# A two-layer decoder trunk on one core: the last tiles, the final norm and the stores by halves of the tokens, and two intermediates kept in PSUM

## Chip, cores, metric

One core of a Trainium2 chip runs the whole program in one launch. The metric is the device time in microseconds, median of three runs.

## What is computed

Two decoder layers over 512 tokens of width 1024, in float32. Each layer is: RMS norm, one input projection, a token mixer beside a memory cross-attention, an output projection added to x, then RMS norm, a SwiGLU feed-forward (width 2816), added to x. A final RMS norm ends it. The parts that the change touches:

```
# lightning indexer of layer 0: one score per query and key, from 8 index heads
logits = einsum('bthd,bsd->bths', q_idx, k_idx)          # 64 wide, after rope
score  = einsum('bths,bth->bts', relu(logits), w_idx)    # then causal mask, top-k keys per query
# rope on the first 16 of 64 features of queries and keys
rot = concat([x1*c - x2*s, x1*s + x2*c])
# feed-forward of the last layer and the end
x = x + (silu(g) * u) @ w_down
y = x * rsqrt(mean(x*x) + eps) * final_norm
```

## The kernel before

Features lie on the 128 partitions, tokens along the free axis: x is eight tiles of 128x512 that stay in SBUF. A matmul in full precision is three passes of a split operand (`mm3`, L169 to L171: high x high, high x low, low x high). Every weight piece is loaded on SP's queue into a ring of four raw buffers, rounded to its high part by ScalarE (`copy`, L148) or VectorE, and its low part is subtracted by VectorE (L163) or GpSimd (L81, in pieces of 256 columns); rings of three high and three low pieces hold the result (`weight`, L157).

**The order.** A string of words per layer (`SEQ`) says in what order units are emitted, and a table (`PLAN`) names for each stage which of the engines takes the next operation of a kind ("V" VectorE, "P" GpSimd, "A" ScalarE). From that the framework builds each engine's queue with a simulated timeline: it may move instructions forward, high-priority ones first, where buffers are free. PSUM tiles of 512 columns are given out by tags with a limit each: "mm" 2, "S" 2, "T" 4, "O" 2. Projections take "mm" and "O" in turn, index tiles "S" and "mm" in turn.

**The start (to about 200 us).** Layer 0 projects four pairs of index queries and the index key, ropes them (`rope`, L309), splits them into stacks (L333), and for each pair of heads and each block of 128 queries multiplies by the keys into PSUM (L633, L634). ScalarE applies relu from PSUM into an SBUF buffer (L636), and VectorE multiplies by the head's weight and adds to the score in SBUF (L641 for the first head, L643). Each of the four pairs makes five PSUM tiles and six multiply-adds, 24 in all, a third each of 256, 384 and 512 columns. When the scores are complete GpSimd multiplies them by the norm's row, and the top-k runs on VectorE: sixteen rounds per block of "eight largest" (L617) and "replace them" (L618), emitted in portions between the other units. The remaining projections, the memory attention and the DSA attention heads follow (L364, L369, L375, L402, L425). Rope shuffles the PSUM result into an SBUF tile b (L312), multiplies the PSUM result by the cosine into a (L313), b by the sine (L314), and adds b to a (L315); the last two go to VectorE or GpSimd by the plan. There are 19 ropes: five in stage 0 with both on VectorE, six in stage 1 with the sine product on GpSimd, eight in layer 1.

**The end.** The second half of layer 1's feed-forward ends with eight down tiles d: 33 matmuls of 512 columns each over eleven activation tiles into one bank (L603), VectorE adds the bank to x (L605), and `absorb` squares the tile and adds the squares up (L215). After the eighth, `final` sums the squares over the partitions with matmuls of one column (L193), makes the inverse root in 13 small VectorE steps (L197 to L205), spreads the column back over the partitions by transposes into PSUM (L212), and for each of eight tiles multiplies x by gain and row (L1014, VectorE) and stores 256 KB (L1015, SP).

Of the kernel before, what the change touches and what calls it, by code (L numbers as in the profile page):

```python
# [11 lines left out]
F32R = mybir.dt.float32r  # L12
I32 = mybir.dt.int32
AF = mybir.ActivationFunctionType
# [16 lines left out]
DOWN_SPLIT = (6, 5)  # L31
BUFS = {"xs": 17, "p": 10, "u": 8, "q": 12, "z": 2, "q1": 8, "qi": 4, "cy": 2, "k": 8, "m": 6, "r": 3, "t": 6, "o": 26, "o2": 6}
RINGS = {"wr": 4, "wh": 3, "wl": 3}
# [32 lines left out]
def r32(ap):  # L66
    return ap.bitcast(F32)
# [25 lines left out]
class Trunk:  # L93
# [215 lines left out]
    def rope(self, ps, tabs, out=None):  # L309
        nc = self.nc  # L310
        a, b = self.slot("t", "ra") if out is None else out, self.slot("t", "rb")
        nc.vector.stream_shuffle(b, ps, SWAP)  # L312
        nc.vector.tensor_mul(a, ps, tabs[0])  # L313
        self.engine("rmul").tensor_mul(b, b, tabs[1])  # L314
        self.engine("radd").tensor_add(a, a, b)  # L315
        return a
# [259 lines left out]
    def ffn(self, i):  # L576
        nc, io = self.nc, self.io
        xs, row = self.xs, None
        for half in range(2):
            acts = []  # L580
            for e in range(NFF // 2):
# [13 lines left out]
                acts.append((hi, lo))  # L595
            for d in range(KC):
                ps = self.ps("mm")
                k = 0
# [7 lines left out]
                if half:  # L606
                    self.absorb(d, 1 if i == 0 else None)


# [14 lines left out]
    def index(self, qs, j, ki, wi, score, first):  # L624

        nc = self.nc
        for heads, b in (((0, 1), 1), ((0,), 2), ((1,), 2), ((0,), 3), ((1,), 3)):
# [3 lines left out]
            for at, e in enumerate(heads):  # L631
                q = qs[e][:, b * P : (b + 1) * P]
                nc.tensor.matmul(ps[:, at * n : at * n + n], q, ki[0][:, :n], start=True, stop=False)  # L633
                nc.tensor.matmul(ps[:, at * n : at * n + n], q, ki[1][:, :n], start=False, stop=True)  # L634
            r = self.slot("u", "relu")
            nc.scalar.activation(r[:, : len(heads) * n], ps[:, : len(heads) * n], AF.Relu)  # L636
# [370 lines left out]

    def final(self):
        nc = self.nc
        with self.tc.high_priority():  # L1010
            row = self.spread(self.rsqrt_mean(self.sums, D, NB), NB)
        for c in range(KC):
            o = self.slot("p", "out")
            nc.vector.scalar_tensor_tensor(o, self.x[c], self.gains[:, 6 * KC + c : 6 * KC + c + 1], row, op0=ALU.mult, op1=ALU.mult)  # L1014
            nc.sync.dma_start(self.io["out"][:, c, :], o)  # L1015

    def run(self):
        self.turn, self.flip, self.comp, self.two, self.ready = False, False, {}, {}, set()
        self.whole = [0] * KC
        self.beside = []  # L1020
        self.plan(0)
        self.setup()
        self.dsa()
        self.ffn(0)
        self.nsa()
        self.ffn(1)
        self.final()

# [77 lines left out]
```

## Time and profile before

| | |
|---|---|
| median of three runs | 1307.31 us (1306.09 to 1307.83) |
| the profiled execution | 1306.26 us, its span 1304.5 us |
| mean granted TensorE clock | 0.971 |
| busy, share of the span | TensorE 95%, VectorE 51%, ScalarE 42%, GpSimd 61% |
| DMA | 108.45 MB, mean 83 GB/s |

The profile is of one execution. Busy time is a sum over stages with different limits; a change is to be judged in its own stage. An engine's waits are put down to what released them. L81 is the helper through which GpSimd's operations go, so these are told apart by their tiles: `stay` weights, `sa` and `sb` stacks, `sc` scores.

### The profile page before, as it was taken

What the parts mean: (1) busy time and instruction counts of PE and PEld (TensorE: products, weight loads), DVE (VectorE), ACT (ScalarE), POOL (GpSimd) and SP (SyncE); (2) the same over time, 40 slices, a digit from 0 to 9 for tenths busy, and PEclk for the clock granted to TensorE, in tenths of its full rate; (3) what the DMA queues carried; (4) which work ended last, traced back from release to release, by engine and by line L of the source; (5) the groups of instructions that cost most, each with busy time, mean ns of one, the idle gap of its engine ahead of it and who ended that gap; (6) DMA issues with size and microseconds to landing.
All of it is one profiled execution on the core that took longest, in us unless ns stands there. A gap on an engine that the chain in (4) does not pass through costs nothing.

```text
span 1304.5 us, 17090 instructions
## 1 busy us (share of the span) xinstructions
PE 1238.6 (95%) x5872; PEld 1024.9 (79%) x5872; DVE 663.2 (51%) x1437; ACT 545.8 (42%) x1053; POOL 801.3 (61%) x1103
## 2 busy tenths in 40 slices
PE   7996889999999999999998998999999999999996
PEld 5775756888888888888887778888788888888885
DVE  6999967543222122223588999997632210122213
ACT  4434678433222222233147767776332322222220
POOL 9988875576553355547466455334886655666573
PEclk9997889999999999999997999999999999999998
DMA  7222000332323433223332101112233323333221
GB/s 246 77 81 80 26 8 23 103 101 94 98 78 89 130 102 97 83 78 99 101 114 65 33 17 52 31 35 81 80 113 97 87 79 119 103 97 93 77 89 65
DMA packets 39239, 108.45 MB, mean 83 GB/s; under 512 B 4720, under 2 KB 8432, under 8 KB 39152
## 3 DMA queue, kind: packets, MB, share of 16 engines
q1 hardware_dynamic: 39152, 107.36, 26.4%
q8 instruction: 46, 0.75, 0.2%
q14 instruction: 41, 0.34, 0.1%
HBM read 105.25 MB, written 2.10 MB: 82 GB/s over the span
## 4 chain that ended last, share of the span: by engine, by line
PE 66%; DVE 21%; POOL 5%; ACT 4%; issue 4%; DMA 0%; DVEq 0%; SPq 0%; POOLq 0%; ACTq 0%
PE ps L171 20%; PE ps L170 20%; PE ps L169 20%; POOL sq L81 2%; DVE p L369 2%; PE ps L425 2%; DVE p L393 2%; DVE sc L618 2%; DVE stay L617 2%; DVE ul L411 2%; POOL stay L81 1%; PE ps L402 1%; ACT p L375 1%; DVE sc L643 1%; DVE rb L312 1%
## 5 line engine op out<-in xcount | busy, mean ns | idle before, releaser
L81 POOL TENSOR_TENSOR stay<-stay,stay 128x256 fp32r<-128x256 f32 (+2 forms) x639 | 471.2, 767 | 312.0 <-ACT stay L148 150.0
L148 ACT CAST stay<-stay 128x1024 fp32r<-128x1024 f32 (+4 forms) x218 | 199.2, 915 | 519.7 <-PE ps L170 400.0
L169 PE MATMUL ps<-xh,stay 128*128 128x512 f32 x912 | 358.6, 393 | 6.1 <-ACT xh L230 6.1
L171 PE MATMUL ps<-xh,stay 128*128 128x512 f32 x912 | 358.8, 394 | 1.0 <-DVE stay L163 0.8
L170 PE MATMUL ps<-xl,stay 128*128 128x512 f32 x912 | 358.5, 394 | 1.0 <-DVE xl L231 1.0
L169 PEld LDWEIGHTS ps<-xh,stay 128*128 128x128 f32 x912 | 173.3, 190 | 41.9 <-ACT xh L230 6.1
L171 PEld LDWEIGHTS ps<-xh,stay 128*128 128x128 f32 x912 | 173.1, 190 | 37.7 <-DVE stay L163 1.9
L170 PEld LDWEIGHTS ps<-xl,stay 128*128 128x128 f32 x912 | 173.1, 190 | 37.1 <-DVE xl L231 1.5
L171 PE MATMUL ps<-fh,stay 128*128 128x512 f32 x352 | 137.1, 389 | 0.0
L170 PE MATMUL ps<-fl,stay 128*128 128x512 f32 x352 | 137.1, 389 | 0.0
L169 PE MATMUL ps<-fh,stay 128*128 128x512 f32 x352 | 137.1, 389 | 0.0
L591 DVE TENSOR_TENSOR fa<-fa,ps 128x512 f32<-128x512 f32 x44 | 30.2, 687 | 183.2 <-PE ps L171 170.6
L605 DVE TENSOR_TENSOR stay<-stay,ps 128x512 f32<-128x512 f32 x32 | 22.1, 690 | 168.4 <-PE ps L171 168.4
L588 DVE TENSOR_TENSOR fa<-ps,row 128x512 f32<-128x512 f32 x44 | 30.2, 691 | 127.2 <-PE ps L171 115.5
L375 ACT ACTIVATE p<-p,stay 128x384 f32<-128x384 f32 (+3 forms) x144 | 80.3, 561 | 34.4 <-DVE stay L369 33.6
L81 POOL TENSOR_TENSOR fa<-fa,row 128x256 f32<-128x256 f32 x88 | 65.7, 768 | 24.1 <-ACT fa L589 24.0
L169 PEld LDWEIGHTS ps<-fh,stay 128*128 128x128 f32 x352 | 66.1, 188 | 13.7
L170 PEld LDWEIGHTS ps<-fl,stay 128*128 128x128 f32 x352 | 66.1, 188 | 13.7
L171 PEld LDWEIGHTS ps<-fh,stay 128*128 128x128 f32 x352 | 66.1, 188 | 13.6
L411 DVE TENSOR_TENSOR ul<-ps,uh 128x512 fp32r<-128x512 f32 (+1 forms) x103 | 62.4, 620 | 12.3 <-ACT uh L410 11.6
L163 DVE TENSOR_TENSOR stay<-stay,stay 128x1024 fp32r<-128x1024 f32 (+4 forms) x38 | 46.4, 1223 | 26.9 <-ACT stay L148 26.1
L410 ACT CAST uh<-ps 128x512 fp32r<-128x512 f32 (+1 forms) x103 | 53.5, 533 | 14.8 <-PE ps L402 13.8
(265 smaller groups left out, 2051.9 us busy)
## 6 DMA issues: line engine op xcount, KB each, us to landing
stay<-in_wf SPq DMA_DIRECT2D x88, 512.0 KB, 3.6
stay<-in_w SPq DMA_DIRECT2D x26, 512.0 KB, 3.5
stay<-in_wd SPq DMA_DIRECT2D x32, 384.0 KB, 3.1
stay<-in_wd SPq DMA_DIRECT2D x32, 320.0 KB, 2.9
mem<-in_memT SPq DMA_DIRECT2D x12, 256.0 KB, 4.0
stay<-in_wo SPq DMA_DIRECT2D x6, 512.0 KB, 3.6
stay<-in_wo SPq DMA_DIRECT2D x16, 192.0 KB, 2.4
stay<-in_xT SPq DMA_DIRECT2D x8, 256.0 KB, 6.2
```

The costliest lines, as they stand in the source:

```text
L81: op(out[:, sl], x[:, sl], y[:, sl])
L148: self.nc.scalar.copy(out, x)
L163: self.engine("w").tensor_sub(lo, raw, r32(hi))
L169: mm(out, lhs[0], rhs[0], start=start, stop=False)
L170: mm(out, lhs[0], rhs[1], start=False, stop=False)
L171: mm(out, lhs[1], rhs[0], start=False, stop=stop)
L369: nc.vector.tensor_tensor_reduce(out=p[:, sl], in0=ps[:, sl], in1=bias, op0=ALU.add, op1=ALU.min, scale=-0.125, scalar=3e38, accum_out=lea ...
L375: self.nc.scalar.activation(p, p, AF.Exp, scale=-1.0, bias=least, accum_out=total)
L410: nc.scalar.copy(hi, ps[:, :w])
L411: nc.vector.tensor_sub(lo, ps[:, :w], r32(hi))
L588: nc.vector.tensor_mul(a, g, row)
L591: nc.vector.tensor_mul(a, a, u)
```

## The change

`rope` multiplies by the cosine first. Where the plan gives the sine product to VectorE, the shuffle writes back into the PSUM tile, the product is made from PSUM, in place if VectorE also adds, else into an SBUF tile. Where it is GpSimd's, only the order of the first two instructions changes. The indexer's relu writes back into its PSUM tile, and VectorE reads it there.

The down tiles 6 and 7 of the last half go through `down_last`: their weights are both prepared first (the second tile's into buffers of their own), then for each half of 256 tokens both tiles are multiplied with 256 columns, added, squared on ScalarE; the half's norm follows, and four products of two tiles each, from gained copies `xg` of x that ScalarE has made tile by tile. In the first half three of these are GpSimd's (`LAST`), which takes the row from a copy in SBUF; in the second all four are VectorE's. Each is stored on SP's queue, 128 partitions x 2 tiles x 256 tokens.

```diff
+HALVED = 2
+LAST = ("PPVP", "VVVV")
     def rope(self, ps, tabs, out=None):
-        a, b = self.slot("t", "ra") if out is None else out, self.slot("t", "rb")
-        nc.vector.stream_shuffle(b, ps, SWAP)
+        a = self.slot("t", "ra") if out is None else out
+        mul, add = self.pick("rmul"), self.pick("radd")
         nc.vector.tensor_mul(a, ps, tabs[0])
-        self.engine("rmul").tensor_mul(b, b, tabs[1])
-        self.engine("radd").tensor_add(a, a, b)
+        if mul == "V":
+            nc.vector.stream_shuffle(ps, ps, SWAP)
+            b = ps if add == "V" else self.slot("t", "rb")
+            nc.vector.tensor_mul(b, ps, tabs[1])
+        else:
+            b = self.slot("t", "rb")
+            nc.vector.stream_shuffle(b, ps, SWAP)
+            self.pool.tensor_mul(b, b, tabs[1])
+        (nc.vector if add == "V" else self.pool).tensor_add(a, a, b)
...
-            r = self.slot("u", "relu")
+            r = ps
             nc.scalar.activation(r[:, : len(heads) * n], ps[:, : len(heads) * n], AF.Relu)
...
             for d in range(KC):
+                if i and half and d == KC - HALVED:
+                    self.down_last(acts)
+                    break
...
+                    if i:
+                        self.last_gain(d, slice(0, S))
+    def last_gain(self, c, sl):
+        if c == 0:
+            self.xg = [self.slot("xg", "xg", w=2 * S).rearrange("p (e t) -> p e t", e=2) for _ in range(KC // 2)]
+        self.nc.scalar.activation(self.xg[c // 2][:, c % 2, sl], self.x[c][:, sl], AF.Copy, scale=self.gains[:, 6 * KC + c : 6 * KC + c + 1])
+    def down_last(self, acts):
+        nc, cs, ws = self.nc, range(KC - HALVED, KC), []
+        for c in cs:
+            k = 0
+            ws.append([])
+            for m in DOWN_SPLIT:
+                if c == cs[0]:
+                    w = self.weight(self.io["wd"][1, 1, c, :, k * P : (k + m) * P], m * P)
+                else:
+                    raw, hi, lo = next(self.rings["wr"])[:, : m * P], *(self.slot("xg", "wx", F32R, 2 * S)[:, : m * P] for _ in range(2))
+                    nc.sync.dma_start(raw, self.io["wd"][1, 1, c, :, k * P : (k + m) * P])
+                    nc.scalar.copy(hi, raw)
+                    self.pool.tensor_sub(lo, raw, r32(hi))
+                    w = hi, lo
+                ws[-1] += [tuple(t[:, e * P : (e + 1) * P] for t in w) for e in range(m)]
+                k += m
+        sq = [self.slot("t", "sq") for c in cs]
+        for h in range(2):
+            sl = slice(h * NM, (h + 1) * NM)
+            for c in cs:
+                ps = self.ps("mm")[:, :NM]
+                for n, w in enumerate(ws[c - cs[0]]):
+                    self.mm3(ps, w, tuple(t[:, sl] for t in acts[n]), n == 0, n == NFF // 2 - 1)
+                with self.tc.high_priority():
+                    nc.vector.tensor_add(self.x[c][:, sl], self.x[c][:, sl], ps)
+                    nc.scalar.activation(sq[c - cs[0]][:, sl], self.x[c][:, sl], AF.Square)
+                    self.last_gain(c, sl)
+            with self.tc.high_priority():
+                row = self.spread(self.rsqrt_mean([t[:, sl] for t in self.sums + sq], D, 2), 2)
+            flat = self.slot("r", "row")[:, :NM]
+            for m in sorted(range(KC // 2), key=lambda m: LAST[h][m], reverse=True):
+                o = self.slot("p", "out").rearrange("p (e t) -> p e t", e=2)
+                wide = lambda t: t[:, None, :].to_broadcast([P, 2, NM])
+                if LAST[h][m] == "V":
+                    nc.vector.tensor_mul(o, self.xg[m][:, :, sl], wide(row))
+                else:
+                    if LAST[h].index("P") == m:
+                        nc.scalar.copy(flat, row)
+                    nc.gpsimd.tensor_mul(o, self.xg[m][:, :, sl], wide(flat))
+                nc.sync.dma_start(self.io["out"][:, 2 * m : 2 * m + 2, sl], o)
-    def final(self):
...
```

The old `final`, shown above, goes.

## Rows read from the trace of the kernel before

**Rows 1.** The page's slices of the span (40 of 32.6 us each, busy share in tenths), TensorE and VectorE.

```profile
PE   7996889999999999999998998999999999999996
...
DVE  6999967543222122223588999997632210122213
```

**Rows 2.** Busy time of each engine in four stretches: us from the span's start, length, then PE, PEld, DVE, ACT, POOL busy (with instruction counts), the granted TensorE clock, DMA share, GB/s.

```profile
27.00:75.00 48.00, 44.57 (x208) 35.81 (x209) 45.98 (x84) 20.49 (x37) 42.57 (x45) 0.93 0.22 67
...
75.00:107.00 32.00, 31.93 (x146) 25.52 (x145) 32.00 (x109) 9.59 (x13) 30.03 (x43) 1.00 0.29 90
...
107.00:170.00 63.00, 47.05 (x237) 37.90 (x236) 62.47 (x171) 39.58 (x121) 55.15 (x87) 0.84 0.14 47
...
200.00:1200.00 1000.00, 978.14 (x4692) 817.29 (x4691) 468.17 (x972) 418.43 (x784) 567.85 (x767) 0.99 0.27 84
```

**Rows 3.** The chain of work that ended last, of the stretch 27 to 170 us alone: shares by engine and line.

```profile
by line: DVE sc L618 17.4%; DVE stay L617 16.0%; DVE sc L643 8.6%; issue 7.7%; DVE ml L231 4.8%; DVE p L369 4.3%; DVE ra L315 4.0%; DVE rb L312 3.6%; DVE stay L510 3.4%; DVE ra L313 3.4%; DVE stay L381 3.2%; DVE stay L163 2.3%; DVE mkl L480
```

**Rows 4.** VectorE's instructions between 20 and 75 us by line and shape: line, operation, out<-in, shapes, count | busy us, mean ns | idle before.

```profile
L643 DVE SCALAR_TENSOR_TENSOR sc<-relu,stay,sc 128x512 f32<-128x512 f32 x7 | 7.6, 1087 | 0.0
...
L643 DVE SCALAR_TENSOR_TENSOR sc<-relu,stay,sc 128x384 f32<-128x384 f32 x7 | 5.9, 840 | 0.0
...
L643 DVE SCALAR_TENSOR_TENSOR sc<-relu,stay,sc 128x256 f32<-128x256 f32 x7 | 5.3, 761 | 0.2
...
L314 DVE TENSOR_TENSOR rb<-rb,sin 128x512 f32<-128x512 f32 x5 | 5.0, 1009 | 0.0
...
L315 DVE TENSOR_TENSOR ra<-ra,rb 128x512 f32<-128x512 f32 x4 | 4.6, 1146 | 0.0
...
L312 DVE STREAM_SHUFFLE rb<-ps 128x512 f32<-128x512 f32 x5 | 3.7, 740 | 0.0
...
L641 DVE TENSOR_SCALAR sc<-relu,stay 128x512 f32<-128x512 f32 x1 | 1.0, 956 | 0.0
...
L641 DVE TENSOR_SCALAR sc<-relu,stay 128x384 f32<-128x384 f32 x1 | 0.9, 891 | 0.0
...
L641 DVE TENSOR_SCALAR sc<-relu,stay 128x256 f32<-128x256 f32 x1 | 0.8, 782 | 0.0
...
L315 DVE TENSOR_TENSOR kk<-kk,rb 128x512 f32<-128x512 f32 x1 | 0.7, 666 | 0.0
```

**Rows 5.** VectorE's instructions of the same kinds between 0 and 180 us that have one operand in PSUM (ps, spread), columns as before.

```profile
L313 DVE TENSOR_TENSOR ra<-ps,cos 128x512 f32<-128x512 f32 x4 | 2.7, 672 | 0.0
...
L497 DVE SCALAR_TENSOR_TENSOR mv<-ps,stay,mv 128x256 fp32r<-128x256 f32 x2 | 0.8, 452 | 0.0
...
L706 DVE SCALAR_TENSOR_TENSOR rw<-rw,stay,spread 128x512 f32<-128x512 f32 x1 | 0.7, 739 | 0.0
```

**Rows 6.** Waits between 27 and 170 us: who waited for whom: us in total, times, longest.

```profile
POOL sc L81 <- DVE sc L643: 4.5, 2, 3.4
...
PE ps L633 <- POOL sb L81: 1.5, 2, 1.2
```

**Rows 7.** TensorE's timeline between 64 and 114 us: start, us, line, operation, shape [idle before it <- releaser].

```profile
69.20 0.43 PE L212 MATMUL spread<-stay 128*128 128x128 f32 x2 [0.40 <-DVE stay L205]
...
113.19 0.58 PE L364 MATMUL ps<-kh,sa 128*128 128x256 f32 x1 [5.91 <-POOL sa L81]
```

**Rows 8.** TensorE's timeline: 256-column matmuls in sequence around 153 us, then the last 512-column matmuls of the last down tile and the column sums behind them.

```profile
152.88 0.28 PE L170 MATMUL ps<-stay,mh 128*128 128x256 f32 x1
...
153.47 0.28 PE L169 MATMUL ps<-stay,mh 128*128 128x256 f32 x1
...
1288.06 0.39 PE L169 MATMUL ps<-fh,stay 128*128 128x512 f32 x1
...
1289.19 0.39 PE L171 MATMUL ps<-fh,stay 128*128 128x512 f32 x1
...
1289.42 0.72 PE L193 MATMUL ssq<-stay,sq 128*128 128x1 f32 x6
```

**Rows 9.** Timeline of all engines after the last down tile.

```profile
1289.62 0.69 DVE L605 TENSOR_TENSOR stay<-stay,ps 128x512 f32<-128x512 f32 x1 [6.79 <-PE ps L171]
...
1290.42 0.63 ACT L221 ACTIVATE sq<-stay 128x512 f32<-128x512 f32 x1 [11.73 <-DVE stay L605]
...
1291.10 1.05 PE L193 MATMUL ssq<-stay,sq 128*128 128x1 f32 x8 [0.74 <-ACT sq L221]
...
1292.19 0.17 DVE L197 TENSOR_SCALAR ssq<-ssq 128x4 f32<-128x4 f32 x1 [1.89 <-PE ssq L193]
...
1294.82 1.11 PE L212 MATMUL spread<-stay 128*128 128x128 f32 x4 [2.67 <-DVE stay L205]
...
1295.97 5.36 DVE L1014 SCALAR_TENSOR_TENSOR out<-stay,spread 128x512 f32<-128x512 f32 x8 [1.21 <-PE spread L212]
```

**Rows 10.** The two nearest rows for a 256-column half: a VectorE addition out of PSUM (L766) and a ScalarE pass out of PSUM (L290): count: ns min/median/max, first and last start, shape.

```profile
L766 DVE TENSOR_TENSOR ho<-ho,ps x24: 395/419/426, 148.6 to 245.6; 64x256 f32<-64x256 f32 x24
...
L290 ACT COPY stay<-spread x1: 374/374/374, 69.7 to 69.7; 128x256 f32<-128x256 f32 x1
```

**Rows 11.** GpSimd's timeline: the last weight piece of the kernel.

```profile
1279.48 1.86 POOL L81 TENSOR_TENSOR stay<-stay,stay 128x256 fp32r<-128x256 f32 x3
```

**Rows 12.** One microsecond while the output is stored, and one while weights in runs of 1 KB are loaded for the last output projection, columns as in Rows 2.

```profile
1299.00:1300.00 1.00, 0.00 (x0) 0.00 (x0) 1.00 (x3) 0.00 (x0) 0.00 (x0) 0.50 1.03 381
...
900.00:901.00 1.00, 1.00 (x8) 0.87 (x7) 0.67 (x1) 0.30 (x1) 0.64 (x2) 1.00 1.07 379
```

More of the change, by code (lines that the diff above doesn't have):

```diff
@@ L31 @@
 DOWN_SPLIT = (6, 5)
-BUFS = {"xs": 17, "p": 10, "u": 8, "q": 12, "z": 2, "q1": 8, "qi": 4, "cy": 2, "k": 8, "m": 6, "r": 3, "t": 6, "o": 26, "o2": 6}
+HALVED = 2
+LAST = ("PPVP", "VVVV")
+BUFS = {"xs": 17, "p": 10, "u": 8, "q": 12, "z": 2, "q1": 8, "qi": 4, "cy": 2, "k": 8, "m": 6, "r": 3, "t": 6, "o": 26, "o2": 6, "xg": 8}
 RINGS = {"wr": 4, "wh": 3, "wl": 3}
@@ L1006, in nsa_second @@
                 self.weighted(o[:, kb * P :], self.vals[:, 2 * br + g, kb], [t[:, cs] for t in parts], br == 0 and kb == 0, False)
-    def final(self):
[L1009 to L1015, printed above, removed]
     def run(self):
@@ L1026, in run @@
         self.ffn(1)
-        self.final()
 def _tiles(w, groups):
```

## The prediction, made before the changed kernel was run

> **What bounds the kernel now.** I read the slices of the page first, then the busy time by stage, the chain of waits of the stretch that stands out, VectorE's instructions there by shape, and last the timeline of the end.
>
> TensorE is full nearly everywhere; VectorE is full only at the start and in the middle [rows 1]. By stages: between 200 and 1200 us TensorE works 978 of 1000 us, so nothing that another engine saves there can show. Between 27 and 170 us VectorE works 45.98 of 48, 32.00 of 32 and 62.47 of 63 us, while TensorE is idle for 3.4, 0.1 and 16 us and its granted clock is 0.84 in the last part [rows 2]. The chain of waits of that stretch names VectorE: the top-k steps (L617, L618), the index accumulation (L643), rope (L312 to L315) [rows 3]. So the first 170 us hang on VectorE's queue and the rest on TensorE, except the end, where each engine waits for the one before it: 11.8 us from the last matmul to the last output multiplication, and 3.2 more to the end of the span at 1304.5 [rows 9].
>
> **Part one: relu and rope in PSUM.** Line 315 shows what is at stake: one addition of two SBUF tensors, 128x512, took 666 ns once and 1146 ns as the mean of four others [rows 4], in a stretch where GpSimd is busy 42.57 of 48 us [rows 2]. With one operand in PSUM the same shape took 672 ns as the mean of four in that stretch (L313) [rows 5]. So an operand in PSUM costs next to nothing of its own and spares what GpSimd's work beside it adds.
>
> *Rope.* In stage 0, five ropes have both choices on VectorE. Their L314 goes from 5.0 to 5 x 0.672 = 3.4 us and their L315 from 4.6 + 0.7 = 5.3 to 3.4: 3.5 us less. The shuffle (five of 740 ns [rows 4]) now writes back into PSUM. No row shows that; between an operation of 672 ns and twice a shuffle I take 740, which it resembles most, so 0. Stage 1's ropes multiply on GpSimd and only change the order of two VectorE instructions: 0. Layer 1's ropes lie where TensorE is 978 of 1000 us busy: 0; without that cover the six that multiply on VectorE would be worth some tenths each.
>
> *Index.* The 21 accumulations cost 7.6 + 5.9 + 5.3 = 18.8 us and the three first multiplications 2.7 [rows 4]. The same instruction with a PSUM operand took 739 ns for 512 columns and 452 for 256 [rows 5]; half way, 600 for 384. New sum: 7 x (0.739 + 0.600 + 0.452) = 12.5, and 1.8 for the three: 7.2 us less. Bounds: 0, if this form does not profit as L313 does; 9, if every one came down to L313's rate of 672 ns for 512 columns. ScalarE's relu writes PSUM instead of SBUF, off the chain: 0.
>
> So VectorE's queue gets 10.7 us shorter before 75 us. The rows put a PSUM operand 6 ns above an SBUF one (672 against 666). [...]
>
> *How much of 10.7 arrives.* Index scores, top-k and the later ropes wait in VectorE's queue, which has no idle time until 170 us, so its work ends 10.7 us earlier if its inputs come. TensorE's part from 75 to 107 us is dense and moves only by the waits before it, 1.5 us for GpSimd's stacks [rows 6]. Then it stands still for 5.91 us for a stack of GpSimd until 113.19 [rows 7]. So TensorE can go on 5.9 + 1.5 = 7.4 us earlier at most. GpSimd, busy 30.03 of 32 us between 75 and 107 [rows 2], waited 4.5 us for the scores of L643 [rows 6]; those it gets back, more only if its contended work shrinks too. Between 4.5 and 7.4 I take 6.0. Bounds: 1.5 (TensorE's waits alone) and 10.7 and about 1.6 more, should the slow matmuls after 113 us vanish (L364, 256 columns, took 0.58 there [rows 7] against 0.28 for as many columns at 153 us [rows 8], and the granted clock of the part is 0.84 [rows 2]).
>
> **Part two: the end by halves.** *Added before the last matmul, on TensorE:* the 66 matmuls of two tiles become 132 of 256 columns. Five steps of the small form took 153.47 - 152.88 = 0.59 us, 0.118 each; five of the large one 1.13, 0.226 each [rows 8]. So 66 x (2 x 0.118 - 0.226) = 0.7 us. The first half's column sums stand in TensorE's queue between the matmuls: three tensors, two blocks, two passes, 12 x 0.12 (six took 0.72 [rows 8]) = 1.4, and two transposes 0.3 (two took 0.43 at 69 us [rows 7]). Together 2.4 us. Behind each of them the second half's matmuls queue up, and everything after waits for these: a stall costs its whole length. Bounds: 0, and 0.74 + 2.67 = 3.4, the two waits at the end today, where nothing covers them [rows 9]. Amid other matmuls the same transposes waited 0.40 us [rows 7]; I take 0.4.
>
> *Removed after the last matmul:* the addition 0.69 to 0.42 and the square 0.63 to 0.37 [rows 9, 10]; the sums from 8 steps to 4, 1.05 to 0.53; the norm's 13 small steps stay; the transposes from four to two, 1.11 to 0.56; the output from eight multiplications to four, 5.36 to 2.68 [rows 9]. Together 4.3 us.
>
> *Covered:* the first half's outputs run beside the second half's 7.8 us of matmuls, three on GpSimd, which has nothing to do after 1281.3 us [rows 11], and their stores go ahead of the others on SP's queue. ScalarE's gain passes (eight tiles) and the second tile's weight casts lie in a stretch where it is a fifth busy; the tile's weights are needed some 4 us earlier, and have buffers of their own instead of waiting for the ring. If GpSimd is late with them, the price is a stall of up to that. The stores have runs of 1 KB instead of 2 KB: the outgoing stream moves 381 GB/s now, and a load with runs of 1 KB moved 379 [rows 12], so 0; bound: 2.7 us if the last megabyte went at half that rate.
>
> Net: 2.4 + 0.4 - 4.3 = -1.5 us, with ends at +1.5 and -1.9 without the store's bound.
>
> **Sum.** The profiled execution took 1306.26 us (1304.5 of span and 1.8 around it): 1306.26 - 6.0 - 1.5 = 1298.8. It lay 1.05 under the median of 1307.31, so as a median 1299.8.
>
> **The rivals.**
> *GpSimd and TensorE keep the pace.* The 75 to 107 us part is full on both [rows 2], and VectorE merely finishes early and idles. Against it: the top-k steps alone are a third of the chain [rows 3] and need no one but VectorE. The front then gives 1.5 and the end, with a stall of both waits' half, 0.2: 1307.31 - 1.7 = 1305.6.
>
> *PSUM does not spare anything.* L643 and the ropes take as long as before, because it is the other operand that waits. Against it: L313 stood at 672 in the midst of the same stretch [rows 5]. Only the end's 1.5 is left: 1305.8.
>
> *PSUM banks run out (slower).* The index tiles were free as soon as ScalarE had read them; now each is held until VectorE's last accumulation on it, and the ropes hold a projection's bank for four instructions instead of two. Twenty index tiles share two "S" and two "mm" banks, and the next projections need "mm" too. VectorE's 14.3 us of index work amid its other work up to 71 us is spread over some 24 us, 1.2 us a tile; if 16 tiles each stop TensorE for that, it loses 19 us, reaches the point at 107 us at about 125 and goes on there 11 to 12 us later than at 113.19. 1307.31 + 11.5 - 1.5 = 1317. It decides once TensorE loses over 7.4 us between 43 and 70 us; below that the wait of 5.91 us and the 1.5 absorb it, and slower by what can be told needs some 12. For it: TensorE has only 3.4 us of room in this stretch [rows 2]. Against it: there are projections to slip in between, and VectorE drains faster than before.
>
> **How the numbers follow.** My forecast 0.55 (its own range 1293 to 1304), pace kept 0.22, nothing spared 0.06, banks 0.09, and 0.08 for more than I forecast, all 10.7 and the vanished slow matmuls and the end at its best: 1307.31 - 12.3 - 1.9 = 1293.1 and below. A measurement of this kernel can tell about 0.2%, 2.6 us: faster is under 1304.7. Faster: 0.54 of the forecast, 0.09 of the pace case, 0.08: 0.71. Same: 0.01, 0.13 and 0.06: 0.20. Slower: 0.09. The range leaves out the bank case and the tail of the best one: 1292.5 to 1307.0.
>
> **What would show it.** L643 at 450 to 740 ns by shape and rope's L314 and L315 successors near 672 beside a busy GpSimd; the first top-k step near 64 to 67 instead of 74.3 us; TensorE's wait at 107 us gone or at 2 us; the end of TensorE's dense part otherwise as it is. At the end: 256-column matmuls every 0.118 us, waits of under 1 us at the first half's sums and transposes, last matmul to last output 7.5 us instead of 11.8. It is wrong if VectorE shows idle time before 170 us, if TensorE waits for VectorE at index or projection matmuls before 70 us, or if the matmuls of the second half stand behind the first half's norm for more than 2 us.

## The result and the profile after

The changed kernel takes 1291.97 us (median of 4 runs, 1291.63 to 1294.74) against 1306.7 for the kernel before (4 runs on the same chip, 1305.81 to 1307.83): ratio 0.9891, 95% interval 0.987 to 0.9911. That is 14.7 us, twice the 7.5 us that were forecast, and 0.5 us below the range. The direction was right; where the time came from was partly not.

The profiled execution of after took 1294.74 us, its span 1292.9 against 1304.5. So 11.6 us can be located in the traces; another 3 lie in which executions were profiled (after's was 2.8 above its median).

The page's slices of after, TensorE and VectorE, as [rows 1]:

```profile
PE   7997878999999999999998899999999999999996
...
DVE  6699976632221122223588999997631210111113
```

The stretches of [rows 2] in after, same columns:

```profile
27.00:75.00 48.00, 46.70 (x222) 38.88 (x222) 37.98 (x100) 22.75 (x39) 40.35 (x53) 0.93 0.25 78
75.00:107.00 32.00, 29.43 (x136) 23.77 (x135) 32.00 (x104) 10.55 (x14) 30.53 (x43) 1.00 0.28 82
107.00:170.00 63.00, 49.95 (x267) 39.26 (x267) 62.50 (x171) 42.88 (x130) 57.13 (x94) 0.92 0.14 43
200.00:1200.00 1000.00, 980.60 (x4708) 820.59 (x4709) 457.31 (x952) 412.29 (x760) 566.64 (x762) 0.99 0.28 84
```

VectorE is now busy for 37.98 of 48 us in the first stretch, where it was 45.98; TensorE rose from 44.57 to 46.70 there. But fixed windows hide where time is won, because everything after slides. Cut both traces at the same instructions instead: the scaling of the index weights (L680, once), the first product of the first gated layer (L588), layer 1's unfolding (L787), the last output-projection addition of layer 1 (L572), and the last product of the second gated layer. I call the stretches start, **front**, first feed-forward, **middle** (layer 1's mixer) and second feed-forward. First the kernel before, then after; columns as in [rows 2]:

```profile
0.00:47.10 47.10, 37.94 (x159) 30.46 (x160) 35.62 (x52) 23.11 (x33) 45.44 (x60) 0.93 0.59 201
47.10:291.50 244.40, 219.02 (x1030) 171.81 (x1029) 193.38 (x481) 133.04 (x306) 187.36 (x271) 0.94 0.19 60
291.50:648.20 356.70, 356.70 (x1585) 295.76 (x1583) 104.57 (x141) 100.42 (x128) 174.99 (x232) 1.00 0.32 97
648.20:931.20 283.00, 263.58 (x1493) 227.26 (x1492) 255.22 (x644) 191.56 (x465) 152.05 (x207) 0.95 0.18 56
931.20:1224.30 293.10, 293.10 (x1304) 243.14 (x1303) 57.95 (x89) 83.59 (x105) 199.07 (x273) 1.00 0.31 95
```

```profile
0.00:47.30 47.30, 38.79 (x158) 30.75 (x158) 31.34 (x52) 22.62 (x33) 44.38 (x63) 0.93 0.59 201
47.30:283.90 236.60, 213.25 (x1030) 170.22 (x1030) 185.08 (x481) 133.09 (x306) 179.14 (x268) 0.96 0.20 62
283.90:640.60 356.70, 356.70 (x1584) 295.53 (x1583) 103.94 (x139) 100.42 (x128) 174.98 (x232) 1.00 0.33 97
640.60:919.90 279.30, 260.88 (x1494) 224.55 (x1493) 252.21 (x647) 191.99 (x465) 151.13 (x207) 0.96 0.18 57
919.90:1213.00 293.10, 293.10 (x1304) 242.95 (x1303) 56.82 (x90) 84.74 (x105) 199.33 (x274) 1.00 0.32 95
```

The two feed-forwards, where TensorE works without a gap, take 356.7 and 293.1 us in both. The front is 7.8 us shorter, the middle 3.7, the rest (1304.5 - 1224.3 = 80.2 against 1292.9 - 1213.0 = 79.9) 0.3, and the start 0.2 longer: 11.6. Note that in the middle VectorE worked 255.22 of the 283.0 us and TensorE 263.58: neither is full there, and the average over 200 to 1200 us concealed it.

VectorE's instructions of after between 20 and 75 us, which answer to [rows 4]:

```profile
L707 DVE SCALAR_TENSOR_TENSOR sc<-ps,stay,sc 128x512 f32<-128x512 f32 x7 | 5.2, 746 | 1.3 <-ACT ps L700 1.2
L707 DVE SCALAR_TENSOR_TENSOR sc<-ps,stay,sc 128x384 f32<-128x384 f32 x7 | 4.3, 609 | 0.0
...
L318 DVE STREAM_SHUFFLE ps<-ps 128x512 f32<-128x512 f32 x5 | 3.5, 691 | 0.0
L320 DVE TENSOR_TENSOR ps<-ps,sin 128x512 f32<-128x512 f32 x5 | 3.4, 689 | 0.0
L707 DVE SCALAR_TENSOR_TENSOR sc<-ps,stay,sc 128x256 f32<-128x256 f32 x7 | 3.3, 478 | 2.2 <-ACT ps L700 2.2
...
L325 DVE TENSOR_TENSOR ra<-ra,ps 128x512 f32<-128x512 f32 x4 | 2.7, 675 | 0.0
...
L325 DVE TENSOR_TENSOR kk<-kk,ps 128x512 f32<-128x512 f32 x1 | 0.7, 670 | 0.0
```

The prices are those forecast: 746, 609 and 478 ns for 739, 600 and 452, and rope's near 672. The last column is new: VectorE waits here, which it did not before. Between 27 and 170 us the waits of after (who waited for whom: us, times, longest), and TensorE's wait that was 5.91 us in [rows 7]:

```profile
DVE stay L744 <- PE ps L743: 4.7, 1, 4.7
...
DVE sc L707 <- ACT ps L700: 3.5, 2, 2.2
```

```profile
107.97 0.39 PE L374 MATMUL ps<-kh,sa 128*128 128x256 f32 x1 [3.54 <-POOL sa L83]
```

Between 43 and 75 us TensorE and VectorE have changed places, before and then after (columns as in [rows 2]):

```profile
43.00:75.00 32.00, 29.58 (x149) 23.69 (x148) 30.30 (x55) 16.17 (x31) 26.84 (x31) 1.00 0.15 50
```

```profile
43.00:75.00 32.00, 31.67 (x162) 26.71 (x161) 23.42 (x66) 16.94 (x31) 24.64 (x36) 1.00 0.22 66
```

TensorE is now full there, 31.67 of 32 us, and VectorE is idle for 8.6. From 75 us on VectorE is full again, 32.00 of 32.

And the end, answering to [rows 9] and [rows 12]: the timeline from the last matmul, and two of the microseconds in which stores drain.

```profile
1280.14 0.28 PE L173 MATMUL ps<-fh,wx 128*128 128x256 f32 x1
1280.26 0.27 PE L214 MATMUL spread<-stay 128*128 128x128 f32 x1
...
1281.18 0.30 PE L214 MATMUL spread<-stay 128*128 128x128 f32 x1
...
1281.59 0.69 DVE L666 TENSOR_TENSOR out<-xg,spread 128x512 f32<-128x512 f32 x1 [0.71 <-PE spread L214]
...
1284.79 0.69 PE L214 MATMUL spread<-stay 128*128 128x128 f32 x2 [2.81 <-DVE stay L207]
1285.52 2.48 DVE L666 TENSOR_TENSOR out<-xg,spread 128x512 f32<-128x512 f32 x4 [0.78 <-PE spread L214]
```

```profile
1289.00:1290.00 1.00, 0.00 (x0) 0.00 (x0) 0.00 (x0) 0.00 (x0) 0.00 (x0) 0.50 1.03 339
1290.00:1291.00 1.00, 0.00 (x0) 0.00 (x0) 0.00 (x0) 0.00 (x0) 0.00 (x0) 0.50 1.03 350
```

From the end of the last matmul (1280.4) to the last output (1288.0) it is 7.6 us, as forecast. But the first half's transposes stand behind the last matmul, although the last VectorE step of that half's norm ended at 1278.4, so no output begins before 1281.59, and the span ends 4.9 us after the last output instead of 3.2.

### The profile page after: what moved, and what is told of

Its sections match the earlier page's. It is cut to its first block, busy times and chain, and to the rows that moved or that the text cites. A ratio compares the mean times of both kernels' runs of the same rounds, so it can differ in the third digit from the quotient of the medians.

```text
span 1292.9 us, 17235 instructions
## 1 busy us (share of the span) xinstructions
PE 1232.4 (95%) x5946; PEld 1024.5 (79%) x5946; DVE 647.6 (50%) x1449; ACT 553.8 (43%) x1067; POOL 791.9 (61%) x1102
## 4 chain that ended last, share of the span: by engine, by line
PE 72%; DVE 17%; POOL 4%; issue 3%; ACT 2%; DMA 1%; SPq 0%; DVEq 0%; POOLq 0%; ACTq 0%
PE ps L173 22%; PE ps L172 22%; PE ps L171 22%; PE ps L435 2%; DVE sc L682 2%; DVE p L379 2%; PE ps L412 2%; DVE stay L681 2%; DVE ul L421 2%; POOL stay L83 2%; POOL sq L83 2%; DVE p L403 1%; PE ps L374 1%; DVE ml L233 1%; PE ps L375 1%
## 5 line engine op out<-in xcount | busy, mean ns | idle before, releaser
L83 POOL TENSOR_TENSOR stay<-stay,stay 128x256 fp32r<-128x256 f32 (+2 forms) x633 | 464.2, 763 | 323.8 <-ACT stay L150 180.2
L172 PE MATMUL ps<-fl,stay 128*128 128x512 f32 (+1 forms) x352 | 134.8, 383 | 0.0
L173 PE MATMUL ps<-fh,stay 128*128 128x512 f32 (+1 forms) x352 | 134.6, 382 | 0.0
L171 PE MATMUL ps<-fh,stay 128*128 128x512 f32 (+1 forms) x352 | 134.6, 382 | 0.0
L385 ACT ACTIVATE p<-p,stay 128x384 f32<-128x384 f32 (+3 forms) x144 | 80.2, 559 | 21.5 <-DVE stay L379 21.0
L173 PEld LDWEIGHTS ps<-fh,stay 128*128 128x128 f32 x352 | 66.1, 188 | 12.8
L412 PE MATMUL ps<-stay,p 128*128 128x128 f32 x360 | 54.1, 275 | 7.0 <-DVE stay L379 3.4
L420 ACT CAST uh<-ps 128x512 fp32r<-128x512 f32 (+1 forms) x103 | 53.3, 533 | 14.2 <-PE ps L412 12.1
```

The source lines that it names most:

```text
L83: op(out[:, sl], x[:, sl], y[:, sl])
L171: mm(out, lhs[0], rhs[0], start=start, stop=False)
L172: mm(out, lhs[0], rhs[1], start=False, stop=False)
L173: mm(out, lhs[1], rhs[0], start=False, stop=stop)
L385: self.nc.scalar.activation(p, p, AF.Exp, scale=-1.0, bias=least, accum_out=total)
L412: nc.tensor.transpose(ps[:, off : off + P], ap, self.ident)
```

## The experiments

**Parts alone.** e1 is the whole change again; e2 its end by halves alone; e3 relu and rope without the end; e4 only this line of the index:

```diff
-            r = self.slot("u", "relu")
+            r = ps
```

> The changed kernel again, for a second profile and a closer ratio. The first profile (span 1292.9) gained 7.6 us before the first feed-forward, 3.7 between that and the second, and 0.3 at the end; the other three runs were 2.8 us faster than the profiled one. If the profile missed nothing: 1292 +-1 us, the same three gains within 1 us. If a part varies from run to run, its gain in this profile differs, by up to 3 us.

> Only the end by halves, relu and rope as before. My theory (the end gives what the profile shows, its own 0.3 us, since the first half's row came late and the stores went slower): 1306.4, no change that can be told. Rival A, my forecast of the end: 1305.2. Rival B (the 2.8 us by which the other runs beat the profiled one lie in the end): 1303.5.

> Only relu and rope in PSUM, the end as before. My theory (front and middle are the change's gain, they add to the end's): 1306.7 - 7.6 - 3.7 = 1295.4, and in the trace the first top-k round near 71 us, the first feed-forward 7.6 us and the second 11.3 us earlier. Rival (the order that the framework makes of each program decides, and the end's part changed it too): above 1298, and other gains in the middle.

> Only the relu in PSUM. VectorE's index work falls from 21.5 to 14.3 us, of 10.7 for both. My theory (VectorE's queue in the front, in proportion): 7.6 x 7.2/10.7 = 5 us in the front, nothing in the middle, which has no relu: 1301.6. Rival (the middle gains from a new order rather than from cheaper ropes): the middle moves here too, by 2 us or more to either side, 1299 or 1304.

| run | us | ratio to before, 95% interval |
|---|---|---|
| e1 whole change | 1292.87 | 0.9897, 0.988 to 0.9913 |
| e2 end alone | 1306.12 | 1.0005, 0.9991 to 1.0019 |
| e3 relu and rope | 1292.72 | 0.9898, 0.9882 to 0.9915 |
| e4 relu alone | 1293.05 | 0.9901, 0.9885 to 0.9917 |

The end by halves is worth nothing that can be told. The relu alone brings the whole gain. My theory expected 1301.6 for e4; it missed by 8.5 us. For e3 it expected 1295.4, 2.7 too much. e1's trace has 9.3 us before the first feed-forward, where the first profile had 7.6, and 3.7 and 0.1 in the other two parts: 13.1 in all, so the first profile missed some of the gain in the start and the front. e5 is e4's kernel again, for its trace.

> The kernel before with only the relu written into its PSUM bank, run again for its profile; layer 1's mixer has the same instructions as in the kernel before. Theory A (VectorE time): the first top-k round and the last index score move by 5 to 8 us, and the rest of the program keeps its pace, so the stretch from the unfolding of layer 1 (648 us before) to the last out-projection (931 us) stays at 283 us. Theory B (order): the framework places layer 1's VectorE instructions in another order, and that stretch is 3 to 4 us shorter, as it is with the whole change.

1293.61 us. The front takes 235.0 us, the middle 281.4. No instruction of layer 1 differs from before in kind; only its order does. So the middle moved by 1.6 us with its order alone, where the order of before, run once more in e10, gave 282.6 for 283.0. That lies between Theory A's 283 and Theory B's 279 to 280.

**VectorE's time or the bank?** e6 leaves the relu in SBUF and shortens the accumulations (`m = n // 2`, score and relu sliced to m columns, so it leaves out half of the index scores); e7 keeps the relu in PSUM and puts a copy behind each accumulation:

```diff
+                nc.vector.tensor_copy(self.slot("u", "relu")[:, :192], self.cs[:, :192])
```

> The kernel before with its relu in SBUF, but the 21 accumulations of the index scores take only the first half of their columns (left out: the other half of the index scores). Their VectorE time then falls by about as much as in the changed kernel (512 columns at 746 ns there; 256 columns in SBUF were 761 ns). Theory A: VectorE's queue in the front is what counts, so the front gains 7 to 8 us and the time is 1298 to 1300, or 1293 if layer 1's order changes with it. Theory C: the gain in the front comes from the PSUM bank (no SBUF buffer, no second read beside GpSimd's), so the time stays at 1305 to 1307.

> The relu alone in PSUM, and after each of the 24 accumulations a copy of 128 x 192 elements from SBUF to SBUF on VectorE that nothing reads, at an estimated 250 to 350 ns each, so that about 6 to 8 us of VectorE's queue come back. Theory A: the front loses what it had gained, and the time goes back to 1301 to 1306. Theory C (the bank, not VectorE): it stays at 1293 to 1295.

e6: 1302.19 us, ratio 0.9957 (0.994 to 0.9974); front 239.3 us, 5.1 less than before. The 21 accumulations took 13.0 us instead of 18.8, so less VectorE time alone, with no PSUM, shortens the front. The time lies between the ranges of the two theories, and GpSimd's work in the front fell too, from 187.36 to 183.88 us. e7: 1304.9 us (0.9983, 0.9969 to 0.9997), which looks like theory A and is not. The copies in the trace (duration min/median/max, first and last start):

```profile
L644 DVE COPY relu<-cos x24: 247/249/784, 16.9 to 29.2; 128x192 f32<-128x192 f32 x24
```

They depend on nothing, so the planner put all of them ahead of the index work. The start became 53.6 us long, the front stayed at 236.2, and the middle came out at 286.1. The run does not test what it was made for.

**Order.** e8 only exchanges the two lines of rope (cosine product first), with nothing in PSUM.

> The kernel before with nothing in PSUM; in rope the product with the cosine is issued ahead of the shuffle, as in the change, and the shuffle still goes to SBUF. Every instruction and its price stay as they were, only the framework's order changes (489 of 677 VectorE instructions of layer 1's mixer keep their order, 395 of 463 in the front). Theory A: 1305 to 1307. Theory B: order alone moves the time by up to 4 us either way, 1302 to 1310, and the stretch from 648 to 931 us with it.

1308.36 us, ratio 1.0011 (1.0 to 1.0022): front 247.8, middle 281.6. To separate order from price properly, e9 fixes the order: the kernel of e4 is planned as it is, and afterwards, in the finished instruction lists, the 20 relus are pointed at SBUF and the 24 accumulations at the same place. Nothing else moves.

```diff
+    for i in block.instructions:          # after the order and the waits are set
+        if relu: outs = [SBUF buffer of this PSUM bank]
+        if accumulation: ins[0] = [the same buffer]
```

> The kernel with the relu alone in PSUM (1293.6 us), every engine's instructions kept in exactly that order with exactly those waits; only the 20 relus now write to SBUF (seven buffers, one for each PSUM bank, stored rounded to fp32r) and the 24 accumulations read them there. Theory A (the price of VectorE's operand): the accumulations cost 1087, 840 and 761 ns again, VectorE's queue is 7 us longer, and the time goes back to 1299 to 1306. Theory B (the gain is the other order): 1293 to 1296.

1298.13 us, ratio 0.9932 (0.9919 to 0.9946); front 239.3, middle 280.7. That is in neither theory's range. Giving the operand back costs 4.3 us in the front at that order. The other 8.7 us to the kernel before looked like order. e13 below did not bear that out for the change itself.

**The clock and TensorE's waits.** TensorE's granted clock is 0.66 of full speed at 110 to 120 us of before, behind the wait of 5.91 us, and 1.00 ahead of it. That is a mix of two readings: in windows of 0.5 us of before it is 1.00 from 107 to 110 us, 0.50 from 110.5 to 117 and 1.00 again from 117.5 to 120, with 0.90 and 0.78 in the two windows between. A 256-column matmul took 0.58 us in the slow part [rows 7] and 0.28 at 153 us [rows 8], where the clock is 1.00 (150 to 160 us). If the slow matmuls were part of the cost, the wait would cost twice. e10 fills two waits of before with matmuls whose results are overwritten, again in the finished lists; e11 does it in after.

> The kernel before with its order and waits unchanged, and 72 matmuls of 128x256 put into TensorE's queue in the front, their results overwritten: 46 ahead of the matmul that waited 5.91 us at 107 us, 26 ahead of the one that waited 3.35 us at 122 us (at 118 ns each 5.4 and 3.1 us). Theory D (clock): the granted clock, 0.66 to 0.83 from 110 to 150 us, stays near 1.0, the same matmuls take some 5 us less, and the time falls to 1299 to 1303. Rival (VectorE or GpSimd sets the pace behind those waits, the clock only fills idle time): 1305 to 1308.

> The whole change with 38 such matmuls put in after its order is set: 26 ahead of the matmul that waited 3.54 us at 104 us, 12 ahead of the one that waited 1.66 us at 117 us. Theory D (clock): the granted clock, 0.84 and 0.68 from 110 to 130 us, stays near 1.0, and the time falls by 1 to 3 us, to 1289 to 1292. Rival: 1292 to 1295.

```profile
110.00:120.00 10.00, 6.81 (x23) 5.52 (x24) 9.86 (x28) 2.92 (x7) 9.69 (x14) 0.66 0.21 72
```

```profile
110.00:120.00 10.00, 9.14 (x45) 7.28 (x43) 9.90 (x27) 3.38 (x7) 9.69 (x14) 1.00 0.20 62
```

The first line is before, the second e10. The clock stays at its upper reading, 1.00 instead of 0.66, and the time does not move: 1306.59 us, ratio 0.9995 (0.9983 to 1.0007). Look at the third figure: VectorE is busy 9.86 and 9.90 of 10 us. With the higher clock the front is no shorter, 244.3 us for 244.4. GpSimd, the fifth figure, is at 9.69 in both, so e10 alone does not tell which of the two sets the pace; the chain of waits of before names VectorE [rows 3]. In e11 the granted clock from 110 to 130 us rose from 0.76 to 0.91 only, and the time is 1293.83: no gain either, and no loss that its interval (0.9886 to 0.9915) can tell from e1's.

**Rope, and the price at the change's own order.** e12 is rope in PSUM without the relu; e13 is e3 with its order and waits fixed and the operands back in SBUF.

> The kernel before with only rope's turned half kept in PSUM. Theory A (price of VectorE's operands): five ropes of the front save 3.5 us of VectorE's queue, layer 1's four as much again in a stage where VectorE is 95% busy: 1301 to 1304. Theory B (order): whatever the framework's new order brings, between 1298 and 1310, as the reordered rope without PSUM gave 1308.4; the stretch from 648 to 931 us then moves by up to 4 us either way.

> The relu and rope change without the end by halves (1292.7 us), every engine's instructions in exactly its order with its waits; only the operands go back to SBUF: the relu's outputs (seven buffers), the turned halves of all five ropes of the front and of three of layer 1's six (the other three stay in PSUM). Theory A (prices, at this order): 4.8 us for the relu, as the earlier run at a fixed order showed, and 3 to 3.5 us for the front's ropes: 1300 to 1301, and the remaining 6 us to 1306.8 are order. Rival (prices don't add, since VectorE waits for TensorE there once it is faster): 1296 to 1298, and 9 us or more are order.

e12: 1298.9 us, ratio 0.993 (0.9912 to 0.9948), front 239.4, middle 279.3. e13: 1306.07 us, ratio 0.9996 (0.998 to 1.0011). e12 is faster than its Theory A allowed (1301 to 1304), inside the wide range of Theory B. For e13 both theories failed: with the change's order and the old operands the kernel is as slow as before. Front and middle of e13, then of e3 (columns as in [rows 2]):

```profile
47.30:291.40 244.10, 218.29 (x1030) 172.30 (x1030) 192.79 (x481) 132.85 (x305) 187.43 (x271) 0.94 0.18 60
648.10:927.50 279.40, 261.23 (x1490) 225.24 (x1489) 252.04 (x646) 191.41 (x464) 150.54 (x205) 0.96 0.18 55
```

```profile
46.20:282.70 236.50, 214.58 (x1030) 171.16 (x1030) 184.55 (x481) 133.10 (x306) 179.25 (x268) 0.96 0.19 62
639.40:919.10 279.70, 261.34 (x1494) 224.78 (x1493) 253.31 (x646) 191.97 (x465) 151.19 (x207) 0.96 0.18 57
```

The same orders, so this is price: 244.1 - 236.5 = 7.6 us of front, with 192.79 - 184.55 = 8.2 us less of VectorE in it, and 1.1 us of start. This order is worth nothing in the front (244.1 against 244.4 before). GpSimd, whose instructions are the same in both, has 187.43 - 179.25 = 8.2 us less work too. Its stack parts between 43 and 75 us, in e13, then in e3 (columns as in [rows 4]; the stretch holds other numbers of them):

```profile
L81 POOL TENSOR_TENSOR sb<-ra,sb 64x256 fp32r<-64x256 f32 x6 | 6.0, 1020 | 0.2
```

```profile
L81 POOL TENSOR_TENSOR sb<-ra,sb 64x256 fp32r<-64x256 f32 x4 | 2.9, 736 | 0.2
```

So here the operands that left SBUF shortened the work of both engines, and how much of the 7.6 us came by GpSimd's share no run separates. In the middle it is the other way round: 279.4 us although three of six turned halves lie in SBUF again.

**How much order alone moves.** e14 and e16 are the kernel before with one buffer changed (`"qi": 5` for 4; `"u": 7` for 8), e15 and e18 are e3 with the same edits.

> The kernel before with five buffers of the kind qi where it had four; no instruction and no price changes, the planner's order does (350 of 463 VectorE instructions of the front and 430 of 677 of layer 1's mixer keep theirs). Theory B (the order is worth up to 8 us by itself): anywhere from 1298 to 1312, off 1306.8 by over 2. Rival (orders differ little unless prices do): 1305 to 1308.5.

> The kernel before with seven buffers of the kind u where it had eight: the front keeps nearly its order (457 of 463 VectorE instructions), layer 1's mixer does not (420 of 677). Theory B: the front's milestones stay, the stretch from the unfolding of layer 1 to its last out-projection (283.0 us) moves by 1 to 4 us, and the time with it, 1302 to 1310. Rival: 1305 to 1308.5, the stretch at 282.5 to 283.5.

> The relu and rope change without the end by halves, with five buffers of the kind qi: a new order of the same instructions. Theory B: off 1292.7 by over 2 either way, 1288 to 1302; by the prices alone (8 us under an average order of the kernel before) rather above than below. Rival: 1291.5 to 1294.5.

> The relu and rope change without the end by halves, with seven buffers of the kind u where it had eight: a third order of the same instructions (316 of 463 VectorE instructions of the front in the order of before, 488 of 677 in layer 1's mixer). Theory A (prices carry the front in any order): the first product of the first gated layer 235 +- 3 us after the first index weights are scaled, and 1289 to 1296. Rival (the order of the change was a lucky one): above 1297.

| run | us | ratio, 95% interval | front | middle |
|---|---|---|---|---|
| e14 before, another order | 1306.28 | 0.9997, 0.9986 to 1.0008 | 242.6 | 282.0 |
| e16 before, another order | 1307.03 | 1.0008, 0.9996 to 1.002 | 243.1 | 284.7 |
| e15 relu and rope, another order | 1290.12 | 0.988, 0.9863 to 0.9896 | 232.6 | 280.6 |
| e18 relu and rope, another order | 1290.4 | 0.9879, 0.9859 to 0.9899 | 235.3 | 278.2 |

With SBUF operands four orders (e8, e13, e14, e16) give 1306 to 1308; with PSUM operands three (e3, e15, e18) give 1290 to 1293. The gain is not a lucky order; e9, with the relu's operand in SBUF, is the one exception (see the open points). By the expectations: e14 stayed with its rival, e16's time did too while its middle moved by 1.7 us as Theory B had it, e15 came out 1.4 us below its rival's range, and e18 inside Theory A's. e15 and e18 are the fastest kernels seen, without the end by halves; they lie some 2 us below the changed kernel, measured on other chips, with intervals that overlap.

**Layer 1 alone.** e17 has rope in PSUM only in layer 1; VectorE's 463 instructions of the front stand as before.

> The kernel before with rope's turned half in PSUM in layer 1 alone; VectorE's and ScalarE's instructions of the front keep the order of before one for one. The front stays at 291.5 us to the first product of the first gated layer. Theory B (layer 1's gain comes with the planner's order of it): the stretch from the unfolding to the last out-projection falls from 283.0 to 279 to 281 us, and the time to 1303 to 1305. Rival (it needs the changed front, or is the price of the three ropes that stayed in PSUM in e13): 283 us and 1306 to 1308, or a fall of under 1 us.

1301.36 us, ratio 0.9959 (0.9944 to 0.9974), faster than Theory B had it; the front ends at 291.3. The middle:

```profile
648.00:926.90 278.90, 260.24 (x1501) 223.51 (x1500) 254.54 (x646) 191.06 (x465) 151.48 (x207) 0.98 0.18 57
```

278.9 us instead of 283.0: layer 1's share needs nothing of the front. What got shorter in it? An instruction that the change does not touch, the scaling of the attention weights, SBUF to SBUF (`scale`, L393 before, L401 in e13), in VectorE's groups between 635 and 940 us; before, then e13:

```profile
L393 DVE TENSOR_SCALAR p<-p,stay 128x512 f32<-128x512 f32 x23 | 14.3, 620 | 0.0
L393 DVE TENSOR_SCALAR p<-p,stay 128x384 f32<-128x384 f32 x23 | 13.0, 566 | 0.0
L393 DVE TENSOR_SCALAR p<-p,stay 128x256 f32<-128x256 f32 x23 | 10.5, 457 | 0.0
L393 DVE TENSOR_SCALAR p<-p,stay 128x128 f32<-128x128 f32 x23 | 9.0, 392 | 0.2
```

```profile
L401 DVE TENSOR_SCALAR p<-p,stay 128x512 f32<-128x512 f32 x23 | 13.4, 581 | 0.0
L401 DVE TENSOR_SCALAR p<-p,stay 128x384 f32<-128x384 f32 x23 | 11.7, 510 | 0.0
L401 DVE TENSOR_SCALAR p<-p,stay 128x256 f32<-128x256 f32 x23 | 9.8, 424 | 0.0
L401 DVE TENSOR_SCALAR p<-p,stay 128x128 f32<-128x128 f32 x23 | 8.0, 348 | 0.2
```

The same 92 instructions take 46.8 us before, 42.9 in e13 and in after, 42.5 in e17 (14.2 + 11.2 + 9.1 + 8.0), 47.6 in e16 (14.5 + 12.7 + 10.9 + 9.5), whose middle is 284.7. Their shapes are the same, so it is what stands beside them that differs, and the trace of before tells what: 53 of the 92 ran while no GpSimd instruction did, 39 beside one. At 384 columns the 13 of the first kind took 402 to 417 ns, whether ScalarE was busy or not; the 10 of the second took 768 in the mean and up to 910. In after 56 run free, and the 36 others cost 21.3 us instead of 26.3.

The 3.9 us are about the size of the middle's gain, but they are not shown to be the whole of it: in e17 VectorE's work as a whole falls only from 255.22 to 254.54 us, and in e8 the 92 take 47.5 us while the middle is 281.6. What the runs do show is a difference between the groups: with all six turned halves of layer 1 in PSUM (after, e3, e12, e15, e17, e18) the middle takes 278.2 to 280.6 us, with all of them in SBUF (before, e2, e5 to e9, e14, e16) 280.7 to 286.1; the means are 279.3 and 283.0, the nearest two (e15, e9) lie 0.1 apart. So the gain goes with the edit and not with one lucky order. Rope's own instructions on VectorE in layer 1 became 1.6 us shorter (18.1 to 16.5 us); e13, with three halves back, has 17.0 and keeps 279.4.

## Why the prediction was half right

*What bounds the front: right.* VectorE's queue does, up to the point where TensorE is full. e6 shows it: 6.7 us less of VectorE's work, with nothing in PSUM, made the front 5.1 us shorter. e10 excludes TensorE's clock (1.00 instead of 0.66 from 110 to 120 us, ratio 0.9995). GpSimd's work shrank beside VectorE's (187.36 to 183.88 us in e6), so its share is not separated.

*The price of an operand: right.* Where the prediction had 6 ns between an operand in PSUM and one in SBUF (672 against 666), the trace of after has 670 ns for kk<-kk,ps against 666 for kk<-kk,rb before [rows 4], 4 ns.

*How much arrives: the ratio right, the size low.* The step "So VectorE's queue gets 10.7 us shorter before 75 us" and "Between 4.5 and 7.4 I take 6.0" gave 56%. VectorE's work from the start to the end of the front fell from 35.62 + 193.38 = 229.0 to 31.34 + 185.08 = 216.4 us, by 12.6, of which 7.6 arrived (7.8 of front less 0.2 of start), 60%. At a fixed order it is 7.6 in the front (e13 against e3). The terms for rope and index came out at 10.4 of 10.7 (3.5 and 6.9); the other 2.2 us lie elsewhere, for instance in tl<-kk,th, which the change does not touch, 1221 and 1127 ns before, 903 and 685 after. Arrival was short by 1.6 us, inside its bounds. The first top-k round came at 71.0 us, 3.3 earlier, not at the 64 to 67 that I had named. What I named as the limit, TensorE's wait at 107 us, was not it: 3.54 us of that wait are left, and the matmul behind it starts 5.2 us earlier (107.97 for 113.19), the rest of the gain coming later. By the busy shares the limit now is TensorE between 43 and 75 us, 31.67 of 32 us: VectorE waits there, for its matmuls (4.7 us) and for ScalarE's relu (3.5), where I had said that a wait of VectorE would prove me wrong. So that 56% came so near to 60% is luck. The rival "GpSimd and TensorE keep the pace" was right that VectorE idles, but put it between 75 and 107 us, where VectorE works 32.00 of 32; its time, 1305.6, is excluded. Two readings were wrong, without a cost that the traces show: VectorE's queue did have idle time, 2.0 of 48 us [rows 2], and GpSimd had squares to make and add after 1281.3 us, until 1285.5; in after it stood idle for 14.7 us before its products.

*Layer 1: wrong.* The failed step is "Layer 1's ropes lie where TensorE is 978 of 1000 us busy: 0". The average is true and useless: the middle inside it has TensorE 263.58 of 283.0 us and VectorE 255.22, and the slices of [rows 1] show VectorE's 8 and 9 there. What the runs showed in place of 0 is 3.7 us. The price I named for the case without that cover, some tenths for each of six ropes, was right: 1.6 us of VectorE's work. The scalings beside GpSimd lost 3.9 us as well, in e13 too, so that part goes by the order, or by the three halves that e13 left in PSUM. How the 3.7 us divide stays open. I never asked what the planner does to a stage that an edit hardly touches: it lays every queue anew.

*The end: wrong in one term.* Forecast -1.5; e2 measured 1.0005, no gain, and the profile shows -0.3. From the last product of the second feed-forward to the end of the last matmul it is 67.4 us instead of 65.3, 2.1 more (2.8 forecast), and from there to the last output 7.6 instead of 11.8, as forecast. "The stores ... a load with runs of 1 KB moved 379, so 0; bound: 2.7" failed: the stores with 1 KB runs moved 339 and 350 GB/s against 381 with 2 KB [rows 12], and began only at 1282.3, because the first half's transposes were queued behind the last matmul. The drain behind the last output grew by 1.7 us.

*The sum.* Against the profiled executions: -7.6 instead of -6.0, -3.7 instead of 0, -0.3 instead of -1.5 make -11.6 instead of -7.5. The rest of the miss, some 3.8 us, is that before was profiled 1.05 us under its median and after 2.8 above its own; e1's trace, with 13.1, puts 1.7 of it into the start and the front. By its number the result belongs to the tail that I gave 0.08, 1293.1 and below, but not by its mechanism: neither all of VectorE's saving arrived nor was the end at its best. Without the middle's 3.7 us, for which I had no term, the measured 1291.97 would have been 1295.7, inside the range. The other rivals fell: PSUM spares 6.9 us in the index at the prices shown (18.8 + 2.7 before, 12.8 + 1.8 after), and no bank shortage stopped TensorE (46.70 of 48 us busy).

*Open.* The parts don't add: relu alone -13, rope alone -8, both -13. In the front that is expected, since TensorE then comes near its own limit: between 43 and 75 us it is busy for 30.7 of 32 us in e5, 30.6 in e12 and 31.67 in after. But e9, an order with the old operands, ran at 1298.1 where four others gave 1306 to 1308, and why is not known. e13's executions spread from 1300.1 to 1309.4, so its trace (1303.64) accounts for 9.4 of the 13.4 us between its median and e3's.

## To carry to other kernels

Cut a trace at instructions and not at round times, and look for the stages hidden in an average: a thousand microseconds of busy TensorE contained 283 in which it had 19 us of gaps, and VectorE worked 255. When an operand leaves SBUF, count what the engine beside it gains as well (GpSimd's 8.2 us here, e13 against e3). Where a planner orders the queues, price an edit at a fixed order (change the operands after planning), and redraw the order once or twice with a neutral edit before believing a gain of a few microseconds; here that spread was 2 to 3 us without the one exception. A wait of TensorE and the clock that it lost cost nothing here, while another engine set the pace (e10: 1306.59 us, ratio 0.9995).

## What the hardware showed unexpectedly

A shuffle in place in PSUM took 691 ns, less than the 740 from PSUM to SBUF. With one operand in PSUM a 128x512 product or sum took 670 to 689 ns (means of groups, 20 to 75 us); the same shape with both in SBUF took 666 at its best and 1146 in the mean of four [rows 4]. The one of 666 ns was not alone either: a subtraction of GpSimd's that began in the same moment (35.12 us) took 1268 ns, the next of its kind 730. There GpSimd paid, and not VectorE. Stores in 1 KB runs went at 339 to 350 GB/s with the DMA engines full (share 1.03), where 1 KB loads had gone at 379.
